# A decoder block on one core: other start addresses for the down projection's operands, and a group's last down product placed ahead of the next block

## The chip, the cores and the metric

The kernel runs on one core of a Trainium2 chip. The metric is the device time of one execution in microseconds (us). Three timed runs of the kernel before gave 2107.08, 2108.17 and 2108.25 us, with a median of 2108.17 us. A further execution was taken with the hardware profiler; all rows below are from it.

## The reference

One decoder block on 512 tokens of width 2048 in float32: a normalised input goes through one projection into two attention mixers, their outputs through one projection and a residual, then a SwiGLU feed-forward layer, a second residual and a last normalisation. The change touches the feed-forward layer, which has 5632 hidden units:

```python
        hn2 = rmsnorm(h, norm2_g[l])
        h = h + (jax.nn.silu(hn2 @ w_gate[l]) * (hn2 @ w_up[l])) @ w_down[l]
    return rmsnorm(h, final_g)
```

`w_gate` and `w_up` are 2048 x 5632, `w_down` is 5632 x 2048.

## The kernel before

**Numbers.** Each float32 operand is split into a high part, which ScalarE (ACT) rounds to the matmul's number type (L178), and a low part, the rest, which VectorE (DVE) subtracts (L192). A product of two such operands is three matmuls, written by `mm` at L304 (high by high), L305 and L306 (high by low and low by high). Products of blocks use a seven-product scheme (Strassen's), so sums and differences of blocks are formed by DVE (L1350 for gate and up weights, L1420 for down weights) or by accumulating DMAs.

**Blocks.** The hidden units are worked in 44 blocks `f` of 128. A block is seven products P1 to P7 in the order of `order(f)`, the first always P1 and the last always P3. Each product is two halves, each half 12 matmuls of 128 x 128 by 256 columns, so a block is 168 matmuls. In these **block products** the weights are the stationary operand (loaded into the array; the profile calls the load PEld) and the activations (`B11`, `T1`, `B21`, `T4` and parts of `ah` and `al`) are the moving operand.

**Groups.** After every four blocks follows a group `p` of **down products**, ten in all (L1442 to L1457). It has four quarters `m`, each of seven halves P1 to P7; a half is 12 matmuls (two token halves `t`, two blocks, three matmuls each), so a group is 28 halves or 336 matmuls. Here the roles are turned: the activations of the finished blocks (`hx`, the last four slots of `ah` and `al`, and a pool tile pair `x3h`, `x3l`) are stationary, and the down weights are moving. The halves stand in a list: a quarter's P4 comes one product into the next quarter, and the last quarter's P4 comes last. The first half of a group is worked before the last product (P3) of the block whose number divides by four, the others after it; the last one, (3, P4), is worked after product P1 of the next block.

**Order.** The order of work is written out by hand: `sched` lists products for TensorE, and `jobs` lists in the same order the weight halves to be split. Before TensorE takes a half, `next_half` splits up to three halves ahead. `later(n, f)` runs a step n halves later, `soon(n, f)` n token halves later. Each engine works its instructions in order. Sums of down products leave PSUM by an ACT copy into a staging tile `stg` (L1700; three buffers of kind a, two of kinds b and c) and an accumulating DMA from GpSimd's queue into `kept_sums` (L1707). Weights come as 512 KB tiles `raw` on SyncE's queue (L135) into five buffers; the next one is issued when a buffer comes free.

**Addresses.** A split weight half lies in one of five tiles `w` of 1088 floats. `wsplit` puts it 16 floats into its tile (`WH`, 64 bytes) or, for jobs marked `even`, 32 floats in (`MH`, 128 bytes); the low part follows 512 floats later. The tiles start at multiples of 256 bytes in the built program. So, written as (start of the stationary operand, start of the moving operand) modulo 256 bytes: block products are at (64, 128), and block products whose half is `even` at (128, 128). The `even` halves are the first half of P1 in blocks 0 and 2, in odd blocks, and in blocks that divide by four. Down products are at (0, 64), since `hx` starts 64 floats past the twelfth slot, `x3` at the start of its tile, and down weights at `WH`.

Of the kernel before, what the change touches and what calls it, by code (L numbers as in the profile page):

```python
# [11 lines left out]
F32 = mybir.dt.float32  # L12
F32R = mybir.dt.float32r
AF = mybir.ActivationFunctionType
OP = mybir.AluOpType

S = 512
D = 2048
KB = D // 128
# [4 lines left out]
PH = 4  # L24
# [11 lines left out]
MH, ML, WH, WL = 32, 32, 16, 16  # L36
# [47 lines left out]
def block_kernel(ctx: ExitStack, tc: tile.TileContext, xt, wst, wdn, smalls, wg, w2c, bias, ident_in, gain_in, out):  # L84
# [3 lines left out]
    pe, act, dve, pool_e, sp = nc.tensor, nc.scalar, nc.vector, nc.gpsimd, nc.sync  # L88

    base = ctx.enter_context(tc.tile_pool(name="base", bufs=1))  # L90
    wp = ctx.enter_context(tc.tile_pool(name="wp", bufs=1))
# [8 lines left out]
    def placed(pool, n, at, **kw):  # L100

        return pool.tile([128, n + 64], F32R, **kw)[:, at:at + n]

    def both(pool, n, at, **kw):

        t = pool.tile([128, 2 * n + 64], F32R, **kw)
        return t[:, at:at + n], t[:, at + n:at + 2 * n]
# [3 lines left out]
    ones = base.tile([128, 32], F32, name="ones")  # L111
    cold = base.tile([128, 512], F32, tag="r", name="cold", bufs=2)[:, :128]
    slot = {x: base.tile([128, KB * S + 64], F32R, name="a" + x) for x in "hl"}
    hx = [slot[x][:, 12 * S + 64:KB * S + 64].rearrange("p (a b) -> p a b", b=S) for x in "hl"]
    ah = slot["h"][:, MH:MH + KB * S].rearrange("p (a b) -> p a b", b=S)
    al = slot["l"][:, ML:ML + KB * S].rearrange("p (a b) -> p a b", b=S)
    dve.memset(ones, 1.0)
# [11 lines left out]
    def load_to(n):  # L129
        while state["dma"] < min(n, len(units)):  # L130
            u = state["dma"]
            t = wp.tile([128, 1024], F32, tag="raw", name="raw", bufs=RB)
            for k in range(2 if u < TWO else 1):
                c = slice(512 * k, 512 * k + 512) if u < TWO else slice(0, 1024)
                sp.dma_start(t[:, c], wst[u][:, c])  # L135
            raws[u] = t
            state["dma"] += 1
            if units[u][0] == "pair" and units[u][4] == 0:
                later(3 if pos["half"] else 0, lambda t=t, u=u: pool_e.dma_start(t[:, :MC], wst[u + 3][:, :MC], accum_op=OP.add))
            if units[u] == ("quad", 0, 1):  # L140
                pool_e.dma_start(t, wst[u + 1], accum_op=OP.add)
# [3 lines left out]
    def turn(tag, n=2):  # L145
        turns[tag] = (turns.get(tag, -1) + 1) % n
        return f"{tag}{turns[tag]}"
# [4 lines left out]
    def proj_block(name="pp"):  # L152
        return bank("proj", name)
# [3 lines left out]
    todo_b = deque()  # L157
    lag = deque()

    def wsplit(even):  # L160
        return both(wp, 512, MH if even else WH, tag=turn("w", 5), name="w")

    class Job:

        def __init__(self, src, prep=None, post=None, load=None, dst=None, even=False, pieces=False):
            self.src, self.prep, self.post, self.load, self.dst, self.even = src, prep, post, load, dst, even
            self.pieces = pieces

        def first(self):
            if self.load:
                self.load()
            if self.prep:
                self.prep()
            self.h, self.l = self.dst() if self.dst else wsplit(self.even)
            for h, l, src, sign in self.parts():
                act.activation(h, src, AF.Copy, scale=sign)  # L178

        def parts(self):  # L180
            at = 0
            for src, sign in self.src() if self.pieces else [(self.src(), 1.0)]:
                c = slice(at, at + src.shape[-1])
                at = c.stop
                yield self.h[:, c], self.l[:, c], src, sign

        def second(self):
            for h, l, src, sign in self.parts():
                if sign < 0:
                    dve.scalar_tensor_tensor(l, src, -1.0, h.bitcast(F32), op0=OP.mult, op1=OP.subtract)  # L190
                else:
                    dve.tensor_tensor(l, src, h.bitcast(F32), op=OP.subtract)  # L192
            if self.post:
                self.post()

    class Twin:


        def __init__(self, subs, even=False):
            self.subs, self.even = subs, even  # L200

        def parts(self):
            for s, sub in enumerate(self.subs):
                c = slice(256 * s, 256 * s + 256)
                yield (self.h[:, c], self.l[:, c]) + sub

        def first(self):
            self.h, self.l = wsplit(self.even)
            for h, l, src, prep, post in self.parts():
                if prep:  # L210
                    prep()
                act.activation(h, src(), AF.Copy)

        def second(self):
            for h, l, src, prep, post in self.parts():
                dve.tensor_tensor(l, src(), h.bitcast(F32), op=OP.subtract)
                if post:
                    post()

    def half_of(u, k):  # L220
        return lambda: raws[u][:, 512 * k:512 * k + 512]
# [232 lines left out]
    for k in range(KB):  # L454
        x = xc.pop(k)
# [883 lines left out]
    def order(f):  # L1339
        return ORDER0 if not f else ORDER1 if f in (1, 5, 9, 13, 17) or 3 < f <= FB - PH and f % PH in (3, 0) else ORDER  # L1340
# [61 lines left out]
    def kept(n):  # L1402
        def f():
            t, m = (("B11", 0), ("", 4), ("T1", 0), ("", 0))[n // 4]
            c = 512 * (m + n % 4)
            return tuple(slot[t + x][:, at + c:at + c + 512] for x, at in (("h", WH), ("l", WL)))
        return f

    DOWN = ("P1", "P4", "P2", "P6", "P5", "P7", "P3")
    second = {}  # L1410

    def quarter(p, m, name):

        u = units.index(("dn", p, 2 * m))

        def q(i):
            return raws[u + i // 2][:, 512 * (i % 2):512 * (i % 2) + 512]

        def comb(o, a, b):
            dve.tensor_tensor(o, a, b, op=OP.add)  # L1420

        def sums13():
            comb(q(0), q(0), q(1))
            comb(q(1), q(1), q(2))

        def sum2():
            second[m] = st["pool"].tile([128, 512], F32, tag="s5", name="s5", bufs=1)
            comb(second[m], q(2), q(0))

        def sum4():  # L1430
            comb(q(3), q(3), second[m])

        n, prep, post = {"P1": (0, None, sums13), "P2": (3, None, None), "P6": (2, sum2, None), "P5": (1, None, None),
                         "P7": (0, None, lambda: load_to(u + RB + 1)), "P3": (3, sum4, None),
                         "P4": (2, None, lambda: load_to(u + RB + 2))}[name]
        return Job(lambda: second[m] if name == "P6" else q(n), prep=prep, post=post)

    def downs(p, items):
        for m, name in items:
            sched.append(("s", p, (m, name)))  # L1440
            jobs.append(quarter(p, m, name))

    st = {}
    sched = []
    for f in range(FB):
        qj = quad_jobs(f, order(f))
        p = f // PH - 1
        for i, name in enumerate(order(f)):
            seq = [(m - (n == "P4"), n) for m in range(4) for n in DOWN if m or n != "P4"] + [(3, "P4")]
            if name == "P3" and f and f % PH == 0:  # L1450
                downs(p, seq[:1])
            sched.append(("q", f, name))
            jobs += qj[2 * i:2 * i + 2]
            if name == "P3" and f and f % PH == 0:
                downs(p, seq[1:-1])
            if name == "P1" and f > PH and f % PH == 1:
                downs(p, seq[-1:])  # L1457
    for nb in range(KB):
        jobs.append(Job(lambda nb=nb: fin[nb // 2][:, 512 * (nb % 2):512 * (nb % 2) + 512], dst=kept(nb),
                        post=(lambda nb=nb: load_fin(nb // 2 + LA + 1)) if nb % 2 else None))  # L1460
# [63 lines left out]
    first = [proj_block("pab") for _ in range(2)]  # L1524
    run_unit([(first[n], ah[:, s, :], al[:, s, :], s == 0, False) for n in range(2) for s in range(4)])
    sets = []
    for s in (0, 1, 2, 3):
        for n in range(2):
# [8 lines left out]
            h, l = sets[n]  # L1537
# [4 lines left out]
    for nb in range(2, KB):  # L1542
        while "hs" not in rest and nb == 4 and not idle():
            step()
        if nb == 2:
            p = third
            run_unit([(p, ah[:, k, :], al[:, k, :], False, k == 7) for k in range(4, 8)])
        else:
            p = out_unit(1, ("proj", "sc", "t")[nb // 2 % 3])
# [89 lines left out]
    for i in range(KB):  # L1639
        nb = PASS2[i]  # L1640
        p = out_unit(0)
# [40 lines left out]
    parts = {}  # L1682
# [224 lines left out]
    def put_away(nb):  # L1907
        pool_e.dma_start(kept_hs[nb], hs[:, nb, :])
        if nb == KB - 1:
            rest["hsp"].close()  # L1910
            st["dnp"] = ExitStack()
            pool = st["pool"] = st["dnp"].enter_context(tc.tile_pool(name="dnp", bufs=1))
            st["x3"] = [placed(pool, 3 * S, 0, name="x3" + x) for x in "hl"]
            for name, x, n in (("P2", 0, 0), ("P3", 0, 1), ("P5", 0, 2), ("P1", 0, 3), ("P6", 1, 0), ("P4", 1, 1), ("P7", 1, 2)):
                parts[name] = tuple((b[:, S * n:S * n + S] if x else a[:, n, :]).rearrange("p (i c) -> p i c", c=256)
                                    for a, b in zip(hx, st["x3"]))
# [16 lines left out]
    for kind, a, b in sched:  # L1933
        if kind == "s":
            h, l = next_half()
# [6 lines left out]
        f, name = a, b  # L1942
        product(f, name)
        if (f, name) in AWAY:
            first, n, at = AWAY[f, name]
            for i in range(n):
                later(at + 8 * i // 5, lambda nb=first + i: put_away(nb))
# [277 lines left out]
```

## Time and profile before

| what | value |
|---|---|
| median of three runs | 2108.17 us |
| profiled execution, its own time | 2109.19 us |
| span of that execution, first to last instruction | 2107.1 us |
| TensorE clock granted over the span | 0.999 |
| blocks with down groups, from the first group to the end of the last block | about 894 to 2054 us of the span |

Rows of the timeline give the start in us from the start of the span, the time of one instruction in us, engine, line, operation, tiles as out<-in, and the shape; a bracket at the end is idle time of the engine ahead of it and what ended it. The time of one matmul (0.28 us here) is the way through the array, and matmuls overlap; the pace is the distance from one start to the next. The tile letters have buffer numbers left out, so all block accumulators but two read `P`.

### The profile page before, as it was taken

The page shows a single profiled execution, that of the slowest core. Times are in us where ns is not written, and L with a number is a line of the kernel's source. Part 1 is how long each engine was busy: PE and PEld are TensorE (multiplying, and loading weights), DVE is VectorE, ACT ScalarE, POOL GpSimd, SP SyncE. Part 2 cuts the span into 40 slices and gives each one's busy share as a digit, 9 for nine tenths or more (in the row PEclk, how much of TensorE's full clock was granted, in tenths as well). Part 3 has the DMA queues.
Part 4 walks back from the last instruction along what each step waited for, and adds up shares of the span by engine and source line. Part 5 has one row for each costly group of instructions (what it writes and reads, how often), then busy time and mean ns, then how long its engine had stood idle before and what let it go on. Part 6 is the DMA issues. An engine that isn't in the chain of part 4 may idle for free.

```text
span 2107.1 us, 43221 instructions
## 1 busy us (share of the span) xinstructions
PE 2091.1 (99%) x16085; PEld 2006.5 (95%) x16085; DVE 1723.8 (82%) x3481; ACT 1335.6 (63%) x3089; POOL 373.0 (18%) x465
## 2 busy tenths in 40 slices
PE   9999999999999999999999999999999999999998
PEld 7789999999988889999999999999999999999996
DVE  6778878788877689979888898878888887878886
ACT  6566666566663355575757666576767666675755
POOL 0011111111120002020302112031312213130320
PEclk9999999999999999999999999999999999999999
DMA  6466665666655335355867758596877869594993
GB/s 241 161 207 163 155 163 143 146 153 163 161 180 170 100 103 188 112 206 165 189 174 176 205 141 204 160 217 147 204 164 181 193 149 211 147 214 112 210 267 110
DMA packets 153058, 360.91 MB, mean 171 GB/s; under 512 B 16400, under 2 KB 54544, under 8 KB 152848
## 3 DMA queue, kind: packets, MB, share of 16 engines
q1 hardware_dynamic: 90432, 244.09, 35.2%
q0 software_dynamic: 61840, 113.21, 29.9%
q8 instruction: 126, 2.06, 0.4%
q10 hardware_dynamic: 576, 0.85, 0.1%
q14 instruction: 84, 0.69, 0.1%
HBM read 274.66 MB, written 76.55 MB: 167 GB/s over the span
## 4 chain that ended last, share of the span: by engine, by line
PE 91%; DVE 3%; DMA 3%; issue 2%; ACT 1%; POOL 0%; SPq 0%; ACTq 0%; POOLq 0%; DVEq 0%
PE P L304 17%; PE P L306 17%; PE P L305 17%; PE pp L306 5%; PE pp L304 5%; PE pp L305 5%; PE pab L300 3%; PE pab L301 3%; PE pab L299 3%; DMA raw<-in_wst_dram 1%; PE pd L305 1%; PE pd L306 1%; PE pd L304 1%; PE pt L971 1%; DVE w L192 1%
## 5 line engine op out<-in xcount | busy, mean ns | idle before, releaser
L192 DVE TENSOR_TENSOR w<-raw,w 128x512 fp32r<-128x512 f32 (+1 forms) x1264 | 823.6, 663 | 183.8 <-ACT w L178 180.0
L178 ACT ACTIVATE w<-raw 128x512 fp32r<-128x512 f32 (+2 forms) x1298 | 749.1, 600 | 302.0 <-DVE raw L1350 119.9
L306 PE MATMUL P<-ah,w 128*128 128x256 f32 x1056 | 293.7, 278 | 0.3 <-DVE w L192 0.3
L304 PE MATMUL P<-ah,w 128*128 128x256 f32 x1056 | 293.8, 278 | 0.0
L305 PE MATMUL P<-al,w 128*128 128x256 f32 x1056 | 293.3, 278 | 0.0
L1707 POOL DMA_DIRECT2D sums<-stg x240 | 200.1, 956 | 371.5 <-ACT stg L1700 370.0
L306 PEld LDWEIGHTS P<-ah,w 128*128 128x128 f32 x1056 | 198.4, 188 | 0.9 <-DVE w L192 0.7
L304 PEld LDWEIGHTS P<-ah,w 128*128 128x128 f32 x1056 | 198.2, 188 | 0.0
L305 PEld LDWEIGHTS P<-al,w 128*128 128x128 f32 x1056 | 197.9, 187 | 0.0
L1350 DVE TENSOR_TENSOR raw<-raw 128x512 f32<-128x512 f32 x270 | 185.4, 687 | 3.2
L304 PE MATMUL pp<-ah,w 128*128 128x256 f32 (+1 forms) x544 | 164.2, 302 | 1.1 <-ACT w L178 0.6
L306 PE MATMUL pp<-ah,w 128*128 128x256 f32 (+1 forms) x544 | 160.3, 295 | 1.5 <-DVE w L192 1.1
L305 PE MATMUL pp<-al,w 128*128 128x256 f32 (+1 forms) x544 | 159.2, 293 | 0.0
L304 PE MATMUL P<-w,ah 128*128 128x256 f32 x560 | 156.6, 280 | 0.9 <-ACT P L1700 0.9
L305 PE MATMUL P<-w,ah 128*128 128x256 f32 x560 | 156.7, 280 | 0.0
L306 PE MATMUL P<-w,al 128*128 128x256 f32 x560 | 156.4, 279 | 0.0
L1700 ACT ACTIVATE stg<-P 128x256 f32<-128x256 f32 x280 | 105.5, 384 | 47.3 <-PE P L306 30.0
L1354 POOL DMA_DIRECT2D raw<-in_wst_dram x42 | 36.1, 861 | 460.5 <-DVE w L192 191.2
L306 PEld LDWEIGHTS pp<-ah,w 128*128 128x128 f32 x544 | 102.3, 188 | 5.9 <-DVE w L192 2.5
L304 PEld LDWEIGHTS P<-w,ah 128*128 128x128 f32 x560 | 105.1, 188 | 1.1 <-ACT P L1700 1.1
L304 PEld LDWEIGHTS pp<-ah,w 128*128 128x128 f32 x544 | 102.7, 189 | 3.2 <-ACT w L178 0.8
L305 PEld LDWEIGHTS P<-w,ah 128*128 128x128 f32 x560 | 105.2, 188 | 0.0
(416 smaller groups left out, 6460.7 us busy)
## 6 DMA issues: line engine op xcount, KB each, us to landing
raw<-in_wst_dram SPq DMA_DIRECT2D x390, 512.0 KB, 4.4
sums<-stg POOLq DMA_DIRECT2D x160, 256.0 KB, 6.9
raw<-in_wst_dram POOLq DMA_DIRECT2D x34, 448.0 KB, 6.8
raw<-in_wst_dram POOLq DMA_DIRECT2D x42, 256.0 KB, 4.5
sums<-stg POOLq DMA_DIRECT2D x80, 128.0 KB, 7.3
xc<-in_xt_dram SPq DMA_DIRECT2D x16, 256.0 KB, 3.7
bias<-in_bias_dram SPq DMA_DIRECT2D x16, 256.0 KB, 4.4
hs<-in_xt_dram SPq DMA_DIRECT2D x16, 256.0 KB, 5.2
```

The lines of the kernel that those rows point to most:

```text
L178: act.activation(h, src, AF.Copy, scale=sign)
L192: dve.tensor_tensor(l, src, h.bitcast(F32), op=OP.subtract)
L299: pe.matmul(o, wh, mh, start=start, stop=False)
L300: pe.matmul(o, wh, ml, start=False, stop=False)
L301: pe.matmul(o, wl, mh, start=False, stop=stop)
L304: pe.matmul(o, wh, mh, start=start, stop=False, skip_group_check=True)
L305: pe.matmul(o, wh, ml, start=False, stop=False, skip_group_check=True)
L306: pe.matmul(o, wl, mh, start=False, stop=stop, skip_group_check=True)
L1350: return lambda: dve.tensor_tensor(o(), o(), x(), op=OP.add)
L1354: return lambda: pool_e.dma_start(o(), wst[u + i][:, 512 * k:512 * k + 512], accum_op=OP.add)
L1700: return lambda: act.activation(o, a, AF.Copy)
L1707: return lambda s=sums[x, t]: pool_e.dma_start(kept_sums[2 * m + t][:, q:q + n, :], s, **how)
```

## The change

Three start addresses are changed, and one line of the schedule. `hx` starts 48 floats past its slot and `x3` 48 floats into its tile: both are at 192 bytes modulo 256. Down weights, and the weights of the last four blocks' down projection (`kept`), start at 0. So down products are at (192, 0) where they were at (0, 64), as are the 180 matmuls of 512 columns in `last()`. And all halves of a group but the first follow the block's P3 directly, the last one, (3, P4), included. The class `Twin`, which nothing uses, is removed. Line numbers shift: `mm` from L304 to L281, the splits from L178 and L192 to L179 and L193, the staging copy from L1700 to L1675.

```diff
-    hx = [slot[x][:, 12 * S + 64:KB * S + 64].rearrange("p (a b) -> p a b", b=S) for x in "hl"]
+    hx = [slot[x][:, 12 * S + 48:KB * S + 48].rearrange("p (a b) -> p a b", b=S) for x in "hl"]
...
-    def wsplit(even):
-        return both(wp, 512, MH if even else WH, tag=turn("w", 5), name="w")
+    def wsplit(even, at=None):
+        return both(wp, 512, (MH if even else WH) if at is None else at, tag=turn("w", 5), name="w")
...
-            self.h, self.l = self.dst() if self.dst else wsplit(self.even)
+            self.h, self.l = self.dst() if self.dst else wsplit(self.even, self.at)
...
-            return tuple(slot[t + x][:, at + c:at + c + 512] for x, at in (("h", WH), ("l", WL)))
+            return tuple(slot[t + x][:, at + c:at + c + 512] for x, at in (("h", 0), ("l", 0)))
...
-        return Job(lambda: second[m] if name == "P6" else q(n), prep=prep, post=post)
+        return Job(lambda: second[m] if name == "P6" else q(n), prep=prep, post=post, at=0)
...
             if name == "P3" and f and f % PH == 0:
-                downs(p, seq[1:-1])
-            if name == "P1" and f > PH and f % PH == 1:
-                downs(p, seq[-1:])
+                downs(p, seq[1:])
...
-            st["x3"] = [placed(pool, 3 * S, 0, name="x3" + x) for x in "hl"]
+            st["x3"] = [placed(pool, 3 * S, 48, name="x3" + x) for x in "hl"]
```

TensorE at the end of a group, before: the last rows of the fourth quarter's P3 (accumulator `P_9189`) and the first of the next block's P1 (`P_9184`, moving operand `B11`; its first half is `even`).

```order
L306 MATMUL P_9189<-w,al 128x256
L304 MATMUL P_9189<-w,ah 128x256
L305 MATMUL P_9189<-w,ah 128x256
L306 MATMUL P_9189<-w,al 128x256
L304 MATMUL P_9184<-B11h,w 128x256
L305 MATMUL P_9184<-B11l,w 128x256
L306 MATMUL P_9184<-B11h,w 128x256
```

The same place in the changed kernel, where `pd` and `P_9185` are the accumulators of the half (3, P4).

```order
L283 MATMUL P_9189<-w,al 128x256
L281 MATMUL P_9189<-w,ah 128x256
L282 MATMUL P_9189<-w,ah 128x256
L283 MATMUL P_9189<-w,al 128x256
L281 MATMUL pd<-w,x3h 128x256
L282 MATMUL pd<-w,x3h 128x256
L283 MATMUL pd<-w,x3l 128x256
```

The half (3, P4) now follows its group, and block products follow it without a down product between them.

TensorE 24 matmuls on, before: the end of P1 of the next block, and the start of (3, P4), which stands between that P1 and the block's second product.

```order
L304 MATMUL P_9184<-B11h,w 128x256
L305 MATMUL P_9184<-B11l,w 128x256
L306 MATMUL P_9184<-B11h,w 128x256
L304 MATMUL pd<-w,x3h 128x256
L305 MATMUL pd<-w,x3h 128x256
L306 MATMUL pd<-w,x3l 128x256
```

The same place in the changed kernel, with the second product's accumulator `P_9186`.

```order
L281 MATMUL P_9184<-B11h,w 128x256
L282 MATMUL P_9184<-B11l,w 128x256
L283 MATMUL P_9184<-B11h,w 128x256
L281 MATMUL P_9186<-T4h,w 128x256
L282 MATMUL P_9186<-T4l,w 128x256
L283 MATMUL P_9186<-T4h,w 128x256
```

The 12 down matmuls between the block's first two products are gone from there.

ACT at the same boundary, before: the staging copies of the group's P3 (`P_9186`, `P_9189`), the splits of the next halves, a copy of the block's P1 (L1963), and the staging copies of (3, P4) (`pd`, `P_9185`).

```order
L1700 ACTIVATE stg<-P_9186 128x256
L1700 ACTIVATE stg<-P_9189 128x256
L178 ACTIVATE w<-raw 128x512 x2
L1963 ACTIVATE P_9187<-P_9184 128x256
L178 ACTIVATE w<-raw 128x512
L1700 ACTIVATE stg<-pd 128x256
L1700 ACTIVATE stg<-P_9185 128x256
L178 ACTIVATE w<-raw 128x512 x4
```

And in the changed kernel:

```order
L1675 ACTIVATE stg<-P_9186 128x256
L1675 ACTIVATE stg<-P_9189 128x256
L179 ACTIVATE w<-raw 128x512
L1675 ACTIVATE stg<-pd 128x256
L1675 ACTIVATE stg<-P_9185 128x256
L179 ACTIVATE w<-raw 128x512 x2
L1938 ACTIVATE P_9187<-P_9184 128x256
L179 ACTIVATE w<-raw 128x512 x4
```

The two staging copies move ahead by two splits and one copy. On DVE one split moves ahead of the block's first two splits and their two sums; the rows of SyncE and GpSimd keep their order.

More of the change, by code (lines that the diff above doesn't have):

```diff
@@ L158, in block_kernel, with __init__ @@
     lag = deque()
-    def wsplit(even):
-        return both(wp, 512, MH if even else WH, tag=turn("w", 5), name="w")
+    def wsplit(even, at=None):
+        return both(wp, 512, (MH if even else WH) if at is None else at, tag=turn("w", 5), name="w")
     class Job:
-        def __init__(self, src, prep=None, post=None, load=None, dst=None, even=False, pieces=False):
+        def __init__(self, src, prep=None, post=None, load=None, dst=None, even=False, pieces=False, at=None):
+            self.at = at
             self.src, self.prep, self.post, self.load, self.dst, self.even = src, prep, post, load, dst, even
@@ L194, in second @@
                 self.post()
[L196 to L218, printed above, removed]
     def half_of(u, k):
```

## The prediction

> **What bounds the kernel now.** I read the page first: the busy shares, the granted clock, and the chain that ended last.
>
> ```profile
> span 2107.1 us, 43221 instructions
> PE 2091.1 (99%) x16085; PEld 2006.5 (95%) x16085; DVE 1723.8 (82%) x3481; ACT 1335.6 (63%) x3089; POOL 373.0 (18%) x465
> ...
> PEclk9999999999999999999999999999999999999999
> ...
> PE 91%; DVE 3%; DMA 3%; issue 2%; ACT 1%; POOL 0%; SPq 0%; ACTq 0%; POOLq 0%; DVEq 0%
> ```
>
> TensorE sets the time, at full clock. Then I asked for the waits of PE and of its weight loads from 850 to 2050 us, where the down groups lie.
>
> ```profile
> PE P L304 <- ACT P L1700: 0.9, 1, 0.9
> PE P L306 <- DVE w L192: 0.3, 1, 0.3
> ...
> PEld P L304 <- ACT P L1700: 1.1, 1, 1.1
> PEld P L306 <- DVE w L192: 0.7, 2, 0.5
> ```
>
> In 1200 us these few waits make 3 us, PE's and PEld's partly the same ones. So it is the **pace** of matmuls that do not wait, the distance from one start to the next, that can give something. I read it in the timeline of PE around the second and third down group, by first rows of stretches whose length the schedule gives.
>
> ```profile
> 1055.38 0.28 PE L304 MATMUL P<-B11h,w 128*128 128x256 f32 x1
> ...
> 1056.74 0.28 PE L304 MATMUL pd<-w,x3h 128*128 128x256 f32 x1
> ...
> 1058.15 0.28 PE L304 MATMUL P<-T4h,w 128*128 128x256 f32 x1
> ...
> 1094.89 0.28 PE L304 MATMUL P<-B11h,w 128*128 128x256 f32 x1
> ...
> 1096.33 0.28 PE L304 MATMUL P<-B11h,w 128*128 128x256 f32 x1
> ...
> 1114.01 0.28 PE L304 MATMUL P<-B11h,w 128*128 128x256 f32 x1
> ...
> 1130.41 0.28 PE L304 MATMUL P<-w,ah 128*128 128x256 f32 x1
> ...
> 1171.40 0.28 PE L304 MATMUL P<-B11h,w 128*128 128x256 f32 x1
> ```
>
> All are 128x256 matmuls, and they run at three paces:
> - 1094.89 to 1096.33, an `even` half at (128, 128), 12 matmuls: 1.44 us, **120.0 ns**.
> - 1096.33 to 1114.01, 156 block matmuls at (64, 128) behind that `even` half: 17.68 us, **113.3 ns**. 1055.38 to 1056.74, the second half of the P1 of block 9, also behind an `even` half: 1.36 us for 12, 113.3.
> - 1056.74 to 1058.15, the half (3, P4) at (0, 64): 1.41 us, 117.5. 1130.41 to 1171.40, a down group with its P3, 12 + 24 + 312 matmuls: 40.99 us, **117.8 ns**.
> - 1058.15 to 1094.89, the rest of block 9 and all of block 10, 144 + 168 = 312 matmuls at (64, 128) again: 36.74 us, **117.8 ns**.
>
> So one pair of addresses runs at 113.3 behind an `even` half, and at 117.8 behind down products. The pace lasts: nothing in 312 matmuls ends it, and the next `even` half does. It is the same at all ten groups.
>
> **The change, part 1: the order.** With (3, P4) ahead of the next block, the `even` half stands behind all down products, and the 12 + 312 block matmuls behind it meet no down address before the next `even` half. Per pair of blocks that is 36.74 - 312 x 0.1133 = 1.38 us, and 13.8 us for ten. PE waits at six places from the first group on, four of them in this fence (a start 0.2 to 0.6 us behind the one before). The first lies inside a pair:
>
> ```profile
> 1413.66 0.38 PE L306 MATMUL P<-ah,w 128*128 128x256 f32 x1
> 1413.88 0.28 PE L304 MATMUL P<-ah,w 128*128 128x256 f32 x1
> ...
> 1602.55 0.39 PE L306 MATMUL P<-ah,w 128*128 128x256 f32 x1 [0.33 <-DVE w L192]
> ...
> 1720.27 0.38 PE L306 MATMUL P<-ah,w 128*128 128x256 f32 x1
> ...
> 894.02 0.47 PE L304 MATMUL P<-w,ah 128*128 128x256 f32 x1
> ```
>
> What an interruption does, block 0 shows, where some small matmuls break in at 809 us; these rows are 12 matmuls apart in each of its two halves:
>
> ```profile
> 807.05 0.28 PE L306 MATMUL P<-ah,w 128*128 128x256 f32 x1
> 808.41 0.28 PE L306 MATMUL P<-ah,w 128*128 128x256 f32 x1
> ...
> 811.99 0.28 PE L305 MATMUL P<-T4l,w 128*128 128x256 f32 x1
> 813.41 0.28 PE L305 MATMUL P<-al,w 128*128 128x256 f32 x1
> ```
>
> 1.36 us ahead of it and 1.42 behind it, at the same (64, 128): 113.3 became 118. So I take it that a wait ends the pace of 113.3 as well. The wait at 1413.66 leaves some 285 matmuls of its pair, 285 x 4.5 ns = 1.3 us. **Part 1: 13.8 - 1.3 = 12.5 us.** What it moves is covered: one split each on ACT and DVE, two staging copies (L1700) and a 128 KB accumulating DMA come about 2.8 us earlier, the tile load that the split triggers too, and SP's and POOL's rows keep their order. The supply must follow a faster TensorE. By windows (us, then busy us of PE, PEld, DVE, ACT and POOL, granted clock, DMA share, GB/s):
>
> ```profile
> 1058.60:1094.70 36.10, 36.10 (x309) 36.10 (x308) 32.27 (x62) 20.31 (x42) 1.74 (x2) 1.00 0.68 191
> 1096.80:1113.90 17.10, 17.10 (x154) 17.10 (x153) 15.34 (x30) 10.88 (x22) 1.73 (x2) 1.00 0.63 157
> 1115.90:1130.30 14.40, 14.40 (x130) 14.40 (x129) 13.32 (x25) 8.42 (x17) 1.70 (x2) 1.00 0.47 110
> 1134.60:1171.30 36.70, 36.70 (x314) 36.70 (x314) 28.80 (x45) 30.42 (x78) 17.29 (x20) 1.00 0.98 216
> ```
>
> In the pair (first row) DVE works 32.27 us; at 113.3 the stretch lasts 34.7 us, 93% busy. The third row is a block that runs at 113.3 with DVE at 13.32 / 14.40 = 93% and without a wait, so DVE hides it. If that cover fails, DVE's lateness adds a wait as at 1413.66: some 0.2 us and the rest of the pair, up to 1.4 us.
>
> **Part 2: the addresses.** No matmul of 256 columns at (192, 0) is in the trace. The floor is 113.3, the fastest pace there is, and the nearest bad row is 120.0. What speaks for 113.3: the distance of the two starts, 192 modulo 256, is that of block products; and (192, 0) is (64, 128) moved by 128 bytes. If what clashes repeats every 128 bytes, then block and down products are one and the same, and crossing from one to the other changes nothing, while the old (0, 64) differs from (64, 128) by 64. If it repeats every 256, the crossing is a step not seen before, and 117.8, which every crossing so far brought, is likely. I take the first.
>
> At 113.3 a group would give 12 + 24 + 312 + 12 = 360 matmuls x 4.5 ns = 1.62 us, 16.2 us for ten. I do not take all of it, for the fourth window shows a second limit: DMA is 98% busy through the 312 matmuls of a group. Its staging shows in the timeline of ACT in the second group, and in PE's row behind it:
>
> ```profile
> 1034.59 0.38 ACT L1700 ACTIVATE stg<-P 128x256 f32<-128x256 f32 x1 [1.94 <-DMA sums<-stg]
> ...
> 1036.88 0.39 PE L304 MATMUL P<-w,ah 128*128 128x256 f32 x1 [0.88 <-ACT P L1700]
> ```
>
> ACT waited 1.94 us for a staging buffer whose DMA had not landed; the copies queued behind it came late, and TensorE, which needs one of them as a start value, stood still. With 36.70 x 0.98 = 36.0 us of DMA work the stretch can shrink by 0.7 us instead of 1.4, unless transfers slip behind the group's end. Taking 0.7, and 48 x 4.5 ns = 0.2 for the matmuls outside the stretch, a group gives 0.95 us. Group 0 starts behind a wait (894.02) and so at 117.8: nothing. The groups behind 1602.55 and 1720.27 lose theirs before it starts: 0.05 each. **Part 2: 7 x 0.95 + 0.1 = 6.8 us**, between 16.2 and, at 120.0 in all 3360 down matmuls, a loss of 3360 x 2.2 ns = 7.4.
>
> The third address, of the 180 matmuls of 512 columns in `last()`:
>
> ```profile
> 2054.68 0.39 PE L304 MATMUL pl<-B11h,ah 128*128 128x512 f32 x1
> ...
> 2060.18 0.39 PE L304 MATMUL pl<-ah 128*128 128x512 f32 x1
> ```
>
> 24 in 5.50 us, 229 ns; between twice 113.3 and twice 120.0 that is 0.5 us less to 2.0 us more. I take 0, the end that is nearer.
>
> The **sum**, against the profiled execution's own 2109.19 us (its span 2107.1 and 2.1 around it): 2109.19 - 12.5 - 6.8 = 2089.9. That execution stands 1.0 us above the median of the runs, 2108.17, so **2089 us**.
>
> The page "TensorE: Matmul & The Clock Gate" of the Trainium skill (Part 2, step-by-step) says that PE has two independent SBUF read ports, one for the moving operand and one for weight loads, so that loading the next weights does not take read bandwidth from the running matmul. By that rule start addresses are worth nothing, and the sum would be 2108. The trace does not agree where it can be read: 113.3, 117.8 and 120.0 ns for the same shape, without waits, in an order that follows the addresses.
>
> **The rivals.**
> - *Order alone* (0.26): the crossing at 192 over 128 puts down products at 117.8 as the old one did. Speaks for it: all crossings into down products so far did so; against it, the distance of 128 bytes. Part 1 stays: 2108.2 - 12.5 = 2095.7.
> - *The new pair is like (128, 128)* (0.06): 120.0 ns, 7.4 us lost: 2103.
> - *The pace is not the addresses'* (0.06): if it comes from what else runs behind a group (DMA at 0.68 against 0.63 in the windows above), the order moves nothing and the time stays at 2108. Against it: the half of 12 behind the `even` half, at 113.3, stands between two slow stretches with the same traffic. The Trainium skill's rule on two ports ("TensorE: Matmul & The Clock Gate", above) would give this result.
> - *Slower* (0.05): the clash of (128, 128) costs 6.7 ns over the floor; were it met twice per matmul at (192, 0), down products would run at 126.7, 3360 x 8.9 ns = 29.9 us more, and with part 1 the time is 2125.6. It decides from (12.5 + 4.2) / 3360 = 5.0 ns above 117.8, at 122.8 ns. No steady pace in these rows is that slow.
>
> **How the numbers follow.** The forecast, both parts, has 0.57, with its own range from 2078 (13.8 + 16.2, no wait in the way) to 2094 (part 2 nearly gone to DMA waits). The other cases follow by their prices. For 8 in 10 the range has to take in *order alone*, and with the bound of 120.0 it ends at 2103: 2078 to 2103. A measurement of this kernel tells about 0.2%, 4.2 us, from no change. Faster by more than that: 0.57 + 0.26 + 0.06 = 0.89; within it 0.06; slower 0.05.
>
> **What would show it.** Part 1 is right if 312 block matmuls behind the `even` half of blocks 9 and 10 take 35.4 us, and wrong at 36.7. Part 2 is right if the first 12 down matmuls of a group take 1.36 us and P3 2.72 behind them; 1.41 and 2.83 is *order alone*, 1.44 the pair of 120. The DMA limit shows as ACT's waits for `sums<-stg` longer than 1.9 us, as PE waits for ACT L1675 inside groups, and as 312 matmuls in more than 35.4 us. The prediction fails if new waits stand at the ends of blocks, where DVE is at 93%, since each would end the pace of 113.3 up to the next `even` half.

## The result and the profile after

| | before | after |
|---|---|---|
| median | 2107.81 us (4 runs) | 2096.61 us (4 runs, 2094.52 to 2100.12) |
| ratio | | 0.9949, 95% interval 0.9932 to 0.9966 |
| profiled execution, its own time | 2109.19 us | 2097.51 us |
| its span | 2107.1 us | 2095.4 us |

The change takes 11.2 us off. The forecast of 2089 is 7.6 us too low, and the time lies 0.9 us from where the rival *order alone* put it, 2095.7. The page of the changed kernel, with the same rows as before:

```profile
span 2095.4 us, 43221 instructions
PE 2079.0 (99%) x16085; PEld 1994.7 (95%) x16085; DVE 1722.6 (82%) x3481; ACT 1335.2 (64%) x3089; POOL 373.8 (18%) x465
...
PE 89%; DVE 4%; DMA 3%; issue 3%; ACT 1%; POOL 0%; SPq 0%; ACTq 0%; POOLq 0%; DVEq 0%
```

TensorE still sets the time, with the same 16085 matmuls in 12.1 us less busy time (2091.1 before). Next the waits from 850 to 2050 us (us in total, times, longest):

```profile
ACT stg L1675 <- DMA sums<-stg: 16.5, 23, 2.2
...
PEld P L281 <- ACT P L1675: 1.5, 2, 1.0
...
PE P L281 <- ACT P L1675: 1.0, 2, 0.8
...
PEld P L281 <- ACT stg L1675: 0.2, 1, 0.2
```

The kernel before has for the first of these rows:

```profile
ACT stg L1700 <- DMA sums<-stg: 17.9, 22, 1.9
```

PE and its weight loads wait 2.7 us where it was 3.0, and ACT's waits for staging buffers are much as before too, so the gain is again one of pace. The timeline of PE around the third group, by the first rows of stretches whose length the schedule gives:

```profile
1053.41 0.28 PE L281 MATMUL P<-B11h,w 128*128 128x256 f32 x1
...
1054.85 0.28 PE L281 MATMUL P<-B11h,w 128*128 128x256 f32 x1
...
1091.57 0.28 PE L281 MATMUL P<-B11h,w 128*128 128x256 f32 x1
...
1127.09 0.28 PE L281 MATMUL P<-w,ah 128*128 128x256 f32 x1
...
1128.50 0.28 PE L281 MATMUL P<-ah,w 128*128 128x256 f32 x1
...
1131.33 0.28 PE L281 MATMUL P<-w,ah 128*128 128x256 f32 x1
...
1169.49 0.28 PE L281 MATMUL P<-B11h,w 128*128 128x256 f32 x1
```

- 1053.41 to 1054.85, the `even` half: 1.44 us for 12, 120.0 ns as before.
- 1054.85 to 1091.57, the 324 block matmuls behind it: 36.72 us, **113.3 ns**. Of these, 312 ran at 117.8 before.
- 1127.09 to 1128.50, the first down half at (192, 0): 1.41 us for 12. The rows ahead of it are at 113.3, so the pace ends at the crossing.
- 1128.50 to 1131.33, P3: 2.83 us for 24, and 1131.33 to 1169.49, the rest of the group with (3, P4): 38.16 us for 324. Both are **117.8 ns**, as before.

So the order works and the addresses do not. The sum can be checked between two instructions that both kernels have, the first matmul that waits in group 0 and the first of `last()`; the third row below is 24 matmuls behind the second:

```profile
894.76 0.47 PE L281 MATMUL P<-w,ah 128*128 128x256 f32 x1
...
2043.04 0.40 PE L281 MATMUL pl<-B11h,ah 128*128 128x512 f32 x1
...
2048.55 0.39 PE L281 MATMUL pl<-ah 128*128 128x512 f32 x1
```

That stretch is 1148.28 us where it was 2054.68 - 894.02 = 1160.66: **12.4 us less**. Ahead of it the profiled execution lost 0.7 us (894.76 against 894.02), and behind it nothing changed: 52.4 us to the end of the span in both, and 5.51 us for the 24 matmuls of 512 columns where it was 5.50.

### The profile page after: what moved, and what is told of

Read it like the earlier page. It is cut to its first block, busy times and chain, and to the rows that moved or that the text cites. A ratio compares the mean times of both kernels' runs of the same rounds, so it can differ in the third digit from the quotient of the medians.

```text
span 2095.4 us, 43221 instructions
## 1 busy us (share of the span) xinstructions
PE 2079.0 (99%) x16085; PEld 1994.7 (95%) x16085; DVE 1722.6 (82%) x3481; ACT 1335.2 (64%) x3089; POOL 373.8 (18%) x465
## 4 chain that ended last, share of the span: by engine, by line
PE 89%; DVE 4%; DMA 3%; issue 3%; ACT 1%; POOL 0%; SPq 0%; ACTq 0%; POOLq 0%; DVEq 0%
PE P L282 17%; PE P L281 17%; PE P L283 17%; PE pp L283 5%; PE pp L281 5%; PE pp L282 5%; PE pab L277 3%; PE pab L276 3%; PE pab L278 3%; DMA raw<-in_wst_dram 1%; DVE w L193 1%; PE pd L282 1%; PE pd L281 1%; PE pd L283 1%; PE pt L948 1%
## 5 line engine op out<-in xcount | busy, mean ns | idle before, releaser
L193 DVE TENSOR_TENSOR w<-raw,w 128x512 fp32r<-128x512 f32 (+1 forms) x1264 | 823.6, 663 | 175.3 <-ACT w L179 170.6
L179 ACT ACTIVATE w<-raw 128x512 fp32r<-128x512 f32 (+2 forms) x1298 | 748.2, 600 | 303.6 <-DVE raw L1327 123.6
L281 PE MATMUL P<-ah,w 128*128 128x256 f32 x1056 | 292.1, 277 | 0.0
L281 PEld LDWEIGHTS P<-ah,w 128*128 128x128 f32 x1056 | 198.2, 188 | 0.0
L281 PE MATMUL pp<-ah,w 128*128 128x256 f32 (+1 forms) x544 | 164.1, 302 | 1.1 <-ACT w L179 0.7
L281 PE MATMUL P<-w,ah 128*128 128x256 f32 x560 | 156.8, 280 | 1.0 <-ACT P L1675 1.0
L1675 ACT ACTIVATE stg<-P 128x256 f32<-128x256 f32 x280 | 105.8, 385 | 48.9 <-PE P L283 32.6
L281 PEld LDWEIGHTS P<-w,ah 128*128 128x128 f32 x560 | 105.2, 188 | 1.5 <-ACT P L1675 1.5
L281 PEld LDWEIGHTS pp<-ah,w 128*128 128x128 f32 x544 | 102.7, 189 | 3.3 <-ACT w L179 0.9
```

What stands on the lines that cost most here:

```text
L281: pe.matmul(o, wh, mh, start=start, stop=False, skip_group_check=True)
L1675: return lambda: act.activation(o, a, AF.Copy)
```

## The experiments

The main theory, A in the expectations, is that the pace of 113.3 lasts until matmuls cross from one pair of start addresses to another, or until TensorE waits, and that an `even` half, whose two starts are equal, brings it back. The rivals are named with each run. In the diffs the changed kernel is the old side unless the text says otherwise. The kernel before stood at 2108.0 us beside the runs e1 to e4, e9 and e10, and at 2107.9 beside e5 to e8.

### e1 and e2: each half of the change alone

e1 keeps the new order and puts the four addresses back:

```diff
-    hx = [slot[x][:, 12 * S + 48:KB * S + 48].rearrange("p (a b) -> p a b", b=S) for x in "hl"]
+    hx = [slot[x][:, 12 * S + 64:KB * S + 64].rearrange("p (a b) -> p a b", b=S) for x in "hl"]
...
-            return tuple(slot[t + x][:, at + c:at + c + 512] for x, at in (("h", 0), ("l", 0)))
+            return tuple(slot[t + x][:, at + c:at + c + 512] for x, at in (("h", WH), ("l", WH)))
...
-        return Job(lambda: second[m] if name == "P6" else q(n), prep=prep, post=post, at=0)
+        return Job(lambda: second[m] if name == "P6" else q(n), prep=prep, post=post, at=WH)
...
-            st["x3"] = [placed(pool, 3 * S, 48, name="x3" + x) for x in "hl"]
+            st["x3"] = [placed(pool, 3 * S, 0, name="x3" + x) for x in "hl"]
```

> The new order with the old addresses, down products at (0, 64). Theory A (the gain is the order's, the addresses gave nothing): blocks 9 and 10 behind the even half at 113.3 ns, down products at 117.8, time within 2 us of the changed kernel's 2096.6, that is 2095 to 2099. Rival B (the new addresses carry part of the gain): the time is at least 3 us above it, 2100 or more.

Measured: 2096.27 us (2094.49 to 2097.49), ratio 0.9942 [0.9925, 0.9958].

e2 keeps the new addresses and puts the old order back:

```diff
             if name == "P3" and f and f % PH == 0:
-                downs(p, seq[1:])
+                downs(p, seq[1:-1])
+            if name == "P1" and f > PH and f % PH == 1:
+                downs(p, seq[-1:])
```

> The new addresses with the old order, (3, P4) behind P1 of the next block. Theory A: block products behind (3, P4) stay at 117.8 ns, and the time is that of the kernel before, 2107 to 2109. Rival B: part of the gain shows, 2105 or less.

Measured: 2107.60 us (10 runs, 2106.67 to 2108.57), ratio 0.9997 [0.9988, 1.0007]. The timeline of PE in e2 at the half (3, P4), which here still stands between P1 and the second product:

```profile
1054.40 0.28 PE L281 MATMUL P<-B11h,w 128*128 128x256 f32 x1
...
1055.76 0.28 PE L281 MATMUL pd<-w,x3h 128*128 128x256 f32 x1
...
1057.18 0.28 PE L281 MATMUL P<-T4h,w 128*128 128x256 f32 x1
...
1093.92 0.28 PE L281 MATMUL P<-B11h,w 128*128 128x256 f32 x1
```

12 block matmuls in 1.36 us, the 12 down ones at (192, 0) in 1.42, then 312 block matmuls in 36.74: one crossing, and the pace is gone for the whole pair, exactly as it was with (0, 64). The order alone gives the whole change; the time with the addresses alone can't be told from that of the kernel before.

### e3: block products at (192, 0) as well

If the crossing is what fails, there must be none. e3 moves the block products to the down products' pair: their weights to 192 (`even` halves to 0), their activations to 0.

```diff
+        for j in r.values():
+            j.at = 0 if j.even else 48
         return [r[p, k] for p in names for k in range(2)]
...
-                                   for x, at in (("h", MH), ("l", ML)))
+                                   for x, at in (("h", 0), ("l", 0)))
...
-        term[name] = tuple(a[:, 4 * i:4 * i + 4, :].rearrange("p a (b c) -> p (a b) c", c=256) for a in (ah, al))
+        term[name] = tuple(slot[x][:, 4 * S * i:4 * S * i + 4 * S].rearrange("p (a c) -> p a c", c=256) for x in "hl")
```

> The changed kernel with the block products of the feed-forward layer at (192, 0) too, and their even halves at (0, 0), so that crossing to down products and back changes no address. Theory A (117.8 is a state that a crossing brings and that lasts): down products run at 113.3 ns from the first group on that is not entered behind a wait, worth 7 us if the DMAs hold the groups back as forecast and 16 us if not: 2080 to 2090. Rival C (down products have 117.8 of their own, from the traffic of their stage or their access order): no gain, 2095 to 2099.

Measured: 2087.37 us (2084.85 to 2089.29), ratio 0.9901 [0.9886, 0.9916]. The timeline of PE in e3, the second group first, then the seventh:

```profile
1009.25 0.28 PE L281 MATMUL P<-w,ah 128*128 128x256 f32 x1
...
1010.61 0.28 PE L281 MATMUL P<-ah,w 128*128 128x256 f32 x1
...
1013.33 0.28 PE L281 MATMUL P<-w,ah 128*128 128x256 f32 x1
...
1033.14 0.38 PE L281 MATMUL P<-w,ah 128*128 128x256 f32 x1 [0.61 <-ACT P L1677]
...
1051.61 0.28 PE L281 MATMUL P<-B11h,w 128*128 128x256 f32 x1
...
1593.08 0.28 PE L281 MATMUL P<-w,ah 128*128 128x256 f32 x1
...
1629.80 0.28 PE L281 MATMUL P<-B11h,w 128*128 128x256 f32 x1
```

Now the first 12 down matmuls take 1.36 us and P3 2.72, the two numbers that the prediction had asked of part 2. The seventh group does its 324 in 36.72 us, 113.3 ns throughout. The second takes 38.28: it runs at 113.3 up to the wait at 1033.14, and behind it 156 matmuls at 117.8. Seven of the nine groups behind group 0 have a wait, four of them at this place, and all seven run at 117.8 behind it. The other two run at 113.3 throughout. What PE waits for at 1033.14 shows in the timeline of ACT and the sums of e3's waits:

```profile
1028.76 0.39 ACT L1677 ACTIVATE stg<-pd 128x256 f32<-128x256 f32 x1 [0.72 <-DMA sums<-stg]
1030.84 0.38 ACT L1677 ACTIVATE stg<-P 128x256 f32<-128x256 f32 x1 [1.70 <-DMA sums<-stg]
```

```profile
ACT stg L1677 <- DMA sums<-stg: 26.6, 34, 1.8
```

ACT waits 26.6 us for staging buffers where it waited 16.5 in the changed kernel. So once nothing is crossed, both other steps of part 2 are there: 113.3 ns at (192, 0), and the staging that limits it.

### e4: equal starts inside the group

One half of each group, (0, P2), the first behind P3, gets its down weights at 192: (192, 192), equal starts as in an `even` half.

```diff
-        return Job(lambda: second[m] if name == "P6" else q(n), prep=prep, post=post, at=0)
+        return Job(lambda: second[m] if name == "P6" else q(n), prep=prep, post=post, at=48 if m == 0 and name == "P2" else 0)
```

> The changed kernel with one half per group, the first behind P3, at (192, 192) instead of (192, 0), as the even halves of block products have both starts alike. Theory A: those 12 matmuls run at 120 ns and the 312 behind them at 113.3, so up to 1.4 us per group: 2083 to 2091 with the DMA limit. Rival C: the 312 stay at 117.8, and the time is 2096 to 2099.

Measured: 2095.47 us (2093.91 to 2097.06), ratio 0.9940 [0.9925, 0.9955]. PE in e4, the half and what follows it in the third group:

```profile
1131.72 0.28 PE L281 MATMUL P<-w,ah 128*128 128x256 f32 x1
...
1133.14 0.28 PE L281 MATMUL P<-w,x3h 128*128 128x256 f32 x1
...
1169.89 0.28 PE L281 MATMUL P<-B11h,w 128*128 128x256 f32 x1
```

12 in 1.42 us, not at 120.0 either, then 312 in 36.75, still 117.8. The median lies 0.5 us below rival C's range and well outside theory A's. So equal starts alone do not bring the pace back, and theory A's second half is too simple. In an `even` half the start of the stationary operand moves and the moving operand stays; here it is the other way round. Whether that is the difference was not tried.

### e7: another pair for the down products

Down products at (128, 192), with the block products at (64, 128) as in the changed kernel. The distance of the two starts is again 192 modulo 256, and the first stationary operand of the down products, at 128, is loaded while the last block activations are read at 128.

```diff
-    hx = [slot[x][:, 12 * S + 48:KB * S + 48].rearrange("p (a b) -> p a b", b=S) for x in "hl"]
+    hx = [slot[x][:, 12 * S + 32:KB * S + 32].rearrange("p (a b) -> p a b", b=S) for x in "hl"]
...
-            return tuple(slot[t + x][:, at + c:at + c + 512] for x, at in (("h", 0), ("l", 0)))
+            return tuple(slot[t + x][:, at + c:at + c + 512] for x, at in (("h", 48), ("l", 48)))
...
-        return Job(lambda: second[m] if name == "P6" else q(n), prep=prep, post=post, at=0)
+        return Job(lambda: second[m] if name == "P6" else q(n), prep=prep, post=post, at=48)
...
-            st["x3"] = [placed(pool, 3 * S, 48, name="x3" + x) for x in "hl"]
+            st["x3"] = [placed(pool, 3 * S, 32, name="x3" + x) for x in "hl"]
```

> The changed kernel (2096.6 us) with down products at (128, 192): the same distance of 192 again, and a crossing into them that loads weights at 128 while operands are read at 128. Theory A (any crossing that changes the addresses ends 113.3): down products at 117.8, 2095 to 2098. Rival D (only some crossings do, and this one, alike in both starts as in an even half, does not): down products at 113.3, 2083 to 2090.

Measured: 2093.99 us (2092.74 to 2096.27), ratio 0.9935 [0.9923, 0.9948]. PE in e7, second group:

```profile
1009.27 0.28 PE L281 MATMUL P<-w,ah 128*128 128x256 f32 x1
...
1010.64 0.28 PE L281 MATMUL P<-ah,w 128*128 128x256 f32 x1
...
1013.46 0.28 PE L281 MATMUL P<-w,ah 128*128 128x256 f32 x1
...
1051.62 0.29 PE L281 MATMUL P<-B11h,w 128*128 128x256 f32 x1
```

This crossing does keep the pace: 12 down matmuls in 1.37 us. The one back into P3, where weights at 64 are loaded while 192 is read, ends it: 24 in 2.82, then 324 in 38.16. So it is not crossing as such that ends the pace; it depends on the addresses, by these two rows perhaps on those that meet there. Theory A, that any crossing ends it, is wrong here, and rival D is right for the crossing in. The time is near theory A's, 1.0 us below its range, since each group also has the crossing into P3.

### e5 and e6: what limits a group at 113.3

Both start from e3. e5 stores the staged sums instead of adding them:

```diff
-            how = {"accum_op": OP.add} if p else {}
+            how = {}
```

> The kernel of e3 (2087.4 us) with the staged sums of every group stored over the earlier ones instead of added to them, so the sum over groups is left out; the bytes that the core writes are the same, the reading of the old sums falls away. Theory A with the DMA limit (what holds the groups back in e3 is ACT waiting for staging buffers whose accumulating DMA has not landed): those waits vanish, the PE waits inside groups (4.0 us in all) with them, and the groups run at 113.3 ns throughout: 2077 to 2082. Rival E (ACT is late by its own work): the PE waits stay, 2085 to 2089.

e6 keeps the sums, and lets kinds a and b share one ring of five buffers instead of three and two; two other tiles of that ring (`t24`, `res`) follow.

```diff
-            sums[x, t] = st["pool"].tile([128, n, 256], F32, tag="stg" + x, name="stg", bufs=bufs)
+            sums[x, t] = st["pool"].tile([128, n, 256], F32, tag="stg" + ("a" if x in "ab" else x), name="stg", bufs=5 if x in "ab" else bufs)
```

> The kernel of e3 with staging kinds a (three buffers) and b (two) in one ring of five, the same memory. Theory L (the limit is the time a kind b buffer is held, about 9.5 us per quarter): reuse comes after 10.2 us or more, waits for sums<-stg shrink, 2081 to 2086. Theory T (the DMA engines have no room left in a group): the waits move to other buffers and the time stays, 2086 to 2089.

Measured: e5 2082.82 us (2079.61 to 2083.40), ratio 0.9878 [0.9865, 0.9891], 0.8 above the range of theory A and 2.2 below that of rival E; e6 2085.02 (2082.82 to 2089.34), ratio 0.9898 [0.9884, 0.9913]. One row of the windows of each for the 324 matmuls of the second group, e5 ahead of e6 (us, then busy us of PE, PEld, DVE, ACT and POOL, clock, DMA share, GB/s):

```profile
1014.90:1051.40 36.50, 36.50 (x325) 36.50 (x324) 29.42 (x47) 32.32 (x82) 11.78 (x22) 1.00 0.71 239
```

```profile
1014.00:1050.50 36.50, 36.50 (x325) 36.50 (x324) 29.42 (x47) 32.14 (x81) 18.21 (x22) 1.00 1.00 230
```

In both the group runs without a wait at 113.3. Without the adding the DMA engines are 71% busy at 239 GB/s; with it, 100% busy at 230. So the adding takes DMA time, and e3's waits for staging came of that (e5 has none); yet with buffers that go to whichever copy needs one, the same DMA work fits behind a TensorE that does not wait. In e6's profile eight of the nine groups behind group 0 run at 113.3 throughout, ACT's waits for staging buffers fall from 26.6 to 11.6 us, as theory L had it, and the one wait of weight loads that is listed comes from the other side, a split by DVE:

```profile
ACT stg L1677 <- DMA sums<-stg: 11.6, 16, 1.6
...
PEld P L283 <- DVE w L193: 0.3, 1, 0.3
```

### e8: fewer `even` halves

With one pair of addresses the `even` halves should hardly be needed, and each costs 12 x 6.7 ns = 0.08 us. From e3, they stay only in blocks 0 and 1 and behind each group:

```diff
-        r["P1", 0].even = f in (0, 2) or f % 2 == 1 or f % PH == 0 and f > 0
+        r["P1", 0].even = f in (0, 1) or f % PH == 1
```

> The kernel of e3 with even halves only in blocks 0 and 1 and in the block behind each group. Theory A (113.3 lasts until something interrupts it): 21 even halves fewer, each 12 matmuls at 119.4 in place of 113.3, is 1.5 us less: 2085 to 2087. Rival F (113.3 decays, or small waits end it often, and the even halves are needed in every block): each block left at 117.8 costs 0.7 us, 2088 to 2100.

Measured: 2090.37 us, but from 2078.69 to 2093.30 over six runs, ratio 0.9907 [0.9889, 0.9924]. The profiled run is the one at 2078.69; PE in it, over the 636 block matmuls between two groups:

```profile
1051.20 0.28 PE L281 MATMUL P<-B11h,w 128*128 128x256 f32 x1
...
1123.28 0.28 PE L281 MATMUL P<-w,ah 128*128 128x256 f32 x1
```

72.08 us, 113.3 ns without an `even` half in between. The other five runs have no profile; a wait there can leave all that follows up to the next group at 117.8, up to 636 x 4.5 ns = 2.9 us each, which fits their spread but was not seen. The expectation of a gain is not borne out: the median lies in rival F's range, and most runs gained nothing over e3. The profiled run shows no decay, so small waits are the likelier half of F.

### e9 and e10: e3 and e6 once more, side by side

> The kernel of e3 once more, beside e10 on one chip, to tell what the shared staging is worth. Expected by theory A with the staging limit: a median of 2086 to 2089 us, with PE waits for ACT's staging copies inside most down groups and 117.8 ns behind them.

> The kernel of e6 once more. If the waits for staging buffers cost what e3's profile shows (some 4 us of waits and some 3 us of lost pace behind them), the median is 2082 to 2085 us, 3 to 6 us below e9. If those waits are only shifted to other places in the runs that are not profiled, it is within 2 us of e9.

Measured: e9 2087.57 us (2084.85 to 2091.87, five runs), ratio 0.9907 [0.9894, 0.9921]; e10 2084.71 (2082.94 to 2090.80, four runs), ratio 0.9896 [0.9882, 0.9909]. The shared staging is 2.4 us lower in median in the first pair of kernels and 2.9 in the second, but the ranges overlap, so a gain from it is likely and not settled; 2.9 is just under the 3 to 6 expected. The waits expected inside most of e9's groups stand in four of the nine behind group 0, with 117.8 behind three of them; in e10's profile one group has a wait for a staging copy, so the shared ring does not end them in every run. Both versions beat the changed kernel, by 9 us and by some 11 to 12.

## Why the prediction was right and wrong

**The bound and the kind of gain** held: TensorE without waits, three paces, a gain from pace alone.

**Part 1 was right, by its own working.** It predicted 35.4 us for 312 matmuls; 324 took 36.72, which is the same 113.3 ns, in nine of ten pairs. Nine pairs at 1.38 are 12.4 us. One pair was taken off for the wait at 1413.66, where a weight load waited for a split by DVE. That wait did not come back, but the tenth pair was lost, as the timeline of PE in blocks 41 to 43 of the changed kernel shows:

```profile
1985.23 0.28 PE L281 MATMUL P<-B11h,w 128*128 128x256 f32 x1
...
1989.43 0.28 PE L282 MATMUL P<-al,w 128*128 128x256 f32 x1
...
2023.23 0.28 PE L281 MATMUL P<-B11h,w 128*128 128x256 f32 x1
...
2024.67 0.28 PE L281 MATMUL P<-B11h,w 128*128 128x256 f32 x1
```

37 matmuls take 4.20 us (113.5), the next 287 take 33.80 (117.8). PE has no gap between them, but the other engines show a wait too short for one. Their timeline, the weight load last:

```profile
1982.56 0.38 ACT L1675 ACTIVATE stg<-P 128x256 f32<-128x256 f32 x1 [1.72 <-DMA sums<-stg]
...
1983.50 0.69 DVE L193 TENSOR_TENSOR w<-raw,w 128x512 fp32r<-128x512 f32 x1 [1.61 <-ACT w L179]
...
1988.70 0.68 DVE L193 TENSOR_TENSOR w<-raw,w 128x512 fp32r<-128x512 f32 x1
...
1989.43 0.19 PEld L283 LDWEIGHTS P<-ah,w 128*128 128x128 f32 x1
```

ACT waited for a staging buffer, so DVE got its next split late; from 1983.50 on it worked without a pause, and ended the split that this load needs at 1989.38. The load follows 55 ns behind. Seven profiles have a visible gap at this place of a block, the kernel before at 1413.66 among them, and there the load stands 54 or 55 ns behind the split; here it stands 117 ns behind the load before it where the pace has 113. So it waited about 4 ns for DVE, and there the pace ended.

The `even` half at 2023.23 did not help either: the 156 behind it, up to 2043.04 above, take 18.37 us, 117.8, which costs 156 x 4.5 ns = 0.7 us against before. It is one of six in the twelve profiles, of 329 behind block 4, that left 117.8 behind them; between each of the six and the last `even` half that had helped lies a wait, but most `even` halves behind a wait do help. From 894 us to `last()`, starts that come more than 126 ns behind the one ahead of them cost 2.5 us over the pace of 117.8 in the kernel before and 2.0 in the changed one. 12.4 - 0.7 + 0.5, and 25 x 4.5 ns = 0.1 for the first matmuls of that pair, is 12.3 us, against 12.4 measured and 12.5 predicted. The kind of loss was foreseen, a wait for DVE inside a pair; that it cost one pair of ten is luck in part. e1, with the same order, lost blocks 17 to 19 instead.

**Part 2 was wrong at one step:** "If what clashes repeats every 128 bytes, then block and down products are one and the same, and crossing from one to the other changes nothing". It does change something: the crossing at 192 over 128 (the first stationary operand of the down products, at 192, is loaded while block activations at 128 are read) ended the pace in every group that was entered at 113.3 (e2 has it too), so the 6.8 us never came. The prediction named the other reading, a period of 256, and priced it as *order alone*; it put 0.57 on the first and 0.26 on the second, although every crossing into down products so far had ended the pace.

**The rest of part 2 was right, and could not show.** (192, 0) is a pair at 113.3, and not one of 120.0 or 126.7: e3 has 36.72 us for 324. Without a crossing e3 is 9.2 us below the changed kernel, where the prediction had 6.8 for this part. The DMA limit was there in the form that was given, ACT waits for `sums<-stg` and PE waits for ACT inside groups. Its size was argued in the wrong way: a share of 0.98 was read as work that cannot be pressed into less time, and e6 shows the 324 matmuls at 113.3 ns at a share of 1.00 without a wait. The price was in the turn of the staging buffers: in e3's second group a wait of 0.61 us, and 156 x 4.5 ns = 0.7 us in the pace behind it.

**The third address** was worth nothing, as taken: 5.51 us against 5.50.

**"A wait ends the pace of 113.3 as well"** is right most of the time. Behind group 0, the twelve profiles have 27 gaps of more than 126 ns in stretches at 113.3; behind 22 of them the matmuls run at 117.8, behind five at 113.3 as before. One of the five is in the timeline of PE in e5, ahead of a group:

```profile
1699.61 0.38 PE L283 MATMUL P<-ah,w 128*128 128x256 f32 x1 [0.30 <-DVE w L193]
...
1702.21 0.28 PE L281 MATMUL P<-w,ah 128*128 128x256 f32 x1
...
1738.93 0.28 PE L281 MATMUL P<-B11h,w 128*128 128x256 f32 x1
```

The 324 behind that wait take 36.72 us, 113.3 ns. Once a wait even brought the pace back: in e2 the rest of a P3 behind a gap at 1600.8 runs at 113.3, after 117.8 ahead of it.

**The covers held in nine pairs of ten.** DVE was forecast as 93% busy in a pair; in the changed kernel's window it is busy 33.32 of 36.60 us,

```profile
1054.90:1091.50 36.60, 36.60 (x325) 36.60 (x325) 33.32 (x63) 21.50 (x45) 1.94 (x3) 1.00 0.65 187
```

91%, and the waits of the changed kernel list none of PE for a split. The one place where the cover failed is the load at 1989.43, and it began with a wait for staging. The pairs' traffic is no cause of the pace: they run at 113.3 at a DMA share of 0.65 now and ran at 117.8 at 0.68 before, and e6 has 113.3 at 1.00, which closes the rival *the pace is not the addresses'*.

**The rule weighed in the prediction**, that loading weights takes no read bandwidth from the matmul (the Trainium skill, "TensorE: Matmul & The Clock Gate", Part 2, step-by-step), gives 2108 for this change and for e3 alike. The chip gave 2096.6 and 2087.4. e3 differs from the changed kernel in start addresses alone. Whether read bandwidth is what the slower pace lacks, no run here shows.

**What stays open:** why a crossing at 128 over 128 keeps the pace and those at 192 over 128, 0 over 128 and 64 over 192 end it; and why some `even` halves fail (2023.23 here) and some waits leave the pace alone.

## What to carry to other kernels

Where an engine has no waits left, read the distance from one start to the next over long stretches: a few per cent can hide in a pace that depends on start addresses and on what ran before. Such a pace is a state, so ask first what ends it and how long the loss lasts, and give operands that take turns one pair of addresses rather than two good ones. When a forecast rests on an untested crossing, and all the tested ones speak against it, take the tested ones.

## What the runs showed of the hardware

- The same 128x256 matmul, without waits and at a clock of 0.999, starts every 113.3, 117.8 or 120.0 ns. The first two are states: 113.3 held over 636 matmuls in e8, and 117.8 over 324 in the third group of the changed kernel.
- A wait often costs more than its length: behind the one of 0.61 us in e3, 156 matmuls were 4.5 ns slower each, 0.7 us; behind the one of about 4 ns in the changed kernel, 287 were, 1.3 us.
- Start addresses decide whether a crossing ends the pace of 113.3: a load at 128 while 128 was read kept it (12 in 1.37 us, e7); at 192 over 128 (12 in 1.41, the changed kernel) and at 64 over 192 (24 in 2.82, e7) it ended.
- With DMAs that add to what is stored, the DMA engines were busy 1.00 of a group's time at 230 GB/s (e6); with plain stores in the same stretch, 0.71 at 239 (e5).
